# Key pages of a paged cache: fetched into a pool of their own instead of the weight ring

## The chip, the cores and the metric

One Trainium2 chip, one of its cores. The metric is the device time of one execution in microseconds (us), lower is better. A core has TensorE (matmuls), VectorE, ScalarE, GpSimd, and SyncE (SP), which here only issues transfers. In rows of the profile these are PE (and PEld for its weight loads), DVE, ACT, POOL and SP.

## The reference, cut to what matters

One layer of a decoder on 256 prompt tokens and 8 sequences of 4 new tokens, 288 columns in all. The keys of the 8 sequences' past lie in a cache of pages (128 rows of 8 heads x 128 values, 512 KB), which a page table picks: 64 pages.

```python
def ffn_half(h, g, wg, wu, wd):
    hn = rms_norm(h, g)
    return h + 0.5 * ((jax.nn.silu(hn @ wg) * (hn @ wu)) @ wd)
...
    hp = ffn_half(hp, norm_ffn1[l], w_ffn1_gate[l], w_ffn1_up[l], w_ffn1_down[l])
    cb, u, q, k, v, logf = mixer_in(hp, norm_mix[l], w_in[l], b_f[l])
...
    k_past = cache_k[page_table].reshape(DB, P, N_HEADS, HEAD_DIM)
    s = jnp.einsum('bqhd,bkhd->bhqk', q, k_all, preferred_element_type=jnp.float32) * SCALE
```

After the first FFN come the mixer (projections, a short convolution, attention of prompt and samples), a second FFN of the same size, a small per-layer embedding and a last norm. All in float32.

## The kernel before

**Weights.** All matmuls keep float32 accuracy by splitting each operand into a high and a low part and adding three products (L298, L299, L300). A weight tile, 512 rows x 256 columns, 512 KB, is loaded by SP into `wraw`. ScalarE rounds half of it to `whi` (L265), VectorE subtracts that for `wlo` (L266). There are 8 raw tiles (tag `raw`) and 5 pairs of halves. A step of the program uses one weight tile: 2 halves, 24 matmuls.

**The FFN.** A pair of output blocks is four steps over w_gate, then four over w_up. On a gate's end VectorE scales it (`tg`, L358), ScalarE applies the silu (`sg`, L360) and GpSimd multiplies by the norm's factor (`sr`, L362). On the up's end VectorE multiplies (`hd`, L367) and splits (`hl`, L370). After 3 or 4 pairs, the down steps add to `h` (L380).

**Key pages.** The keys must be turned before they can be used. While the first FFN runs, `k_turn(j)` handles page j: GpSimd gathers it by row indices `idx` into a tile `page` (L250), VectorE transposes it by blocks of 32 x 32 into `kt` (L460), and GpSimd writes `kt` with four transfers to `KD` in DRAM (L462). The mixer loads `KT` from `KD` (L247, SP). A page takes one of the 8 raw tiles, like a weight, and one place in the list of loads that runs 8 ahead (`load_upto`). The 64 calls are put among the steps of the FFN, 3.2 steps apart, by numbers at L475.

**The order.** Each engine runs its own queue in order and waits at an instruction until what it needs is there. Which order that is, is settled when the program is built: a scheduler places the instructions, close to the order in which they are written but not the same, so a moved call can move others. TensorE's order is the same before and after. Memory is taken by pools that are opened and closed as a stack from two ends (`opened`, `closed`). The pool `kt` on the right, from step 200 on, holds `KT`.

Of the kernel before, what the change touches and what calls it, by code (L numbers as in the profile page):

```python
# [16 lines left out]
F32 = mybir.dt.float32  # L17
# [8 lines left out]
P = 128  # L26
# [3 lines left out]
DB = 8  # L30
# [4 lines left out]
NH = 8  # L35
CB = 8
PAGES = 8
# [12 lines left out]
TSTEP = 16  # L50
# [38 lines left out]
def build(nc, tc, ctx, A, O):  # L89
    def pool(name, bufs=1, to=ctx, **k):  # L90
        return to.enter_context(tc.tile_pool(name=name, bufs=bufs, reuse_waits="tile", **k))

    v, s, g, pe, sy = nc.vector, nc.scalar, nc.gpsimd, nc.tensor, nc.sync
# [25 lines left out]
    h = cst.tile([P, KT, NT], F32, name="h")  # L119
# [39 lines left out]
    idx = cst.tile([P, 64], I32, name="idx")  # L159
# [73 lines left out]
    steps = []  # L233
# [39 lines left out]
    def page(src, j):  # L273
        return dict(kind="p", src=src, rows=idx[:, j:j + 1])
# [114 lines left out]
    W = {}  # L389

    def opened(name, side="left"):
        st = ExitStack()
        W[name] = (pool(name, to=st, side=side), st)

    def closed(name):
        W.pop(name)[1].close()
# [54 lines left out]

    KD = drp.tile([DB * PAGES // 2, P, 2, 4, NH * 32], F32, name="KD")

    def k_turn(j):

        its = [page(A["cache_k"], j)]

        def fn():
            t = W["f1"][0].tile([P, 4, NH, 32], F32, name="kt", tag="kt", bufs=2)
            v.transpose(t, its[0]["tile"].rearrange("p (h d c) -> p d h c", d=4, c=32))  # L460
            for i in range(4):
                g.dma_start(KD[j // 2, :, j % 2, i].rearrange("(d c) n -> c d n", c=32),  # L462
                            t[32 * i:32 * i + 32].rearrange("c d h r -> c d (h r)"))
        return (its, fn)

    def later_loads():
        t = load_gains(["norm_mix", "norm_ffn2", "norm_ple", "norm_final", "norm_conv_out", "norm_attn_out", "conv_w"], 16, sy)
# [1 line left out]
        defer(lambda: turn_gains(*t), 20)  # L469

    steps.insert(14, ([], lambda: closed("xs")))
    steps.insert(200, ([], lambda: opened("kt", "right")))
    steps.insert(44, ([], later_loads))
    for j in reversed(range(DB * PAGES)):
        steps.insert(66 + TSTEP * j // 5, k_turn(j))  # L475

    warm = cst.tile([P, 1], F32, name="warm")
    v.memset(warm, 1.0)
# [695 lines left out]
```

## Time and profile before

| | us |
|---|---|
| median of 3 runs | 2425.11 (2424.34 to 2426.46) |
| the profiled execution | 2432.94 |
| its span, first to last instruction | 2431.2 |
| TensorE busy | 2375.8 |
| VectorE busy | 1427.1 |
| GpSimd busy | 503.4 |
| transposes of key pages, 64 | 79.7 |
| fetches of key pages, 64 | 76.3 |
| writes to KD, 256 | 142.8 |

The profiled execution is one run of its own and a little longer than the runs timed without a profile. A group's busy time sums what its instructions took on their engine. For a transfer that is the time to issue it; its landing is told apart.

### The profile page before, as it was taken

How to read it: one execution, taken by the hardware profiler on the slowest of the kernel's cores; microseconds unless marked ns; L12 is line 12 of the kernel's file. 1: busy time of each engine (PE TensorE's matmuls, PEld its weight loads, DVE VectorE, ACT ScalarE, POOL GpSimd, SP SyncE). 2: the span in 40 equal slices, each digit the busy share in tenths (PEclk: the TensorE clock that was granted, in tenths of full speed). 3: DMA queues.
4: the chain of work that ended last, by engine and by line, in shares of the span. 5: the costliest groups of instructions: out<-in, count | busy, mean ns of one | idle time of the engine just before them, and what ended most of it. 6: DMA issues, size and time to landing. Idle time of an engine off the chain costs nothing.

```text
span 2431.2 us, 46137 instructions
## 1 busy us (share of the span) xinstructions
PE 2375.8 (98%) x17856; PEld 2298.6 (95%) x17856; DVE 1427.1 (59%) x2588; ACT 1052.2 (43%) x1858; POOL 503.4 (21%) x688
## 2 busy tenths in 40 slices
PE   8999999999999999999999999999999999999997
PEld 8999999999999999888877899999999999999997
DVE  6556655556565577555555685555555555555765
ACT  5443343343443354333334454444444444444554
POOL 2003432333333312111444410000000000000100
PEclk9999999999999999999999999999999999999998
DMA  7457878777777755898787754545555555555542
GB/s 229 154 177 260 295 249 273 239 256 256 243 262 252 245 182 165 295 304 305 244 301 258 258 163 147 177 151 179 165 165 165 166 165 165 165 165 165 165 153 83
DMA packets 410704, 510.85 MB, mean 210 GB/s; under 512 B 22236, under 2 KB 379316, under 8 KB 406356
## 3 DMA queue, kind: packets, MB, share of 16 engines
q1 hardware_dynamic: 376596, 401.43, 52.2%
q0 software_dynamic: 33664, 106.13, 12.4%
q8 instruction: 140, 2.29, 0.4%
q14 instruction: 80, 0.66, 0.1%
q10 hardware_dynamic: 224, 0.34, 0.1%
HBM read 469.19 MB, written 38.63 MB: 209 GB/s over the span
## 4 chain that ended last, share of the span: by engine, by line
PE 71%; DMA 9%; issue 4%; DVE 3%; POOL 1%; ACT 0%; DVEq 0%; POOLq 0%; ACTq 0%
PE mm L298 22%; PE mm L300 22%; PE mm L299 21%; DMA page<-in_cache_k_dram,idx 6%; DMA KD<-kt 2%; PE va L719 1%; PE va L776 1%; DVE wlo L266 1%; POOL KD L462 1%; DMA page<-in_cache_v_dram,idx 1%; DVE kt L460 1%; PE va L298 1%; PE va L300 1%; PE va L299 1%; ACT whi L265 0%
## 5 line engine op out<-in xcount | busy, mean ns | idle before, releaser
L266 DVE TENSOR_TENSOR wlo<-wraw,whi 128x512 fp32r<-128x512 f32 x1384 | 964.3, 706 | 645.1 <-ACT whi L265 601.8
L265 ACT ACTIVATE whi<-wraw 128x512 fp32r<-128x512 f32 x1384 | 862.0, 630 | 994.3 <-PE mm L299 930.6
L298 PE MATMUL mm<-xh,whi 128*128 128x288 f32 x3712 | 1110.5, 299 | 5.5 <-DVE hd L367 3.5
L300 PE MATMUL mm<-xh,wlo 128*128 128x288 f32 x3712 | 1094.2, 295 | 10.2 <-DVE wlo L266 10.2
L299 PE MATMUL mm<-xl,whi 128*128 128x288 f32 x3712 | 1097.1, 296 | 0.0
L298 PEld LDWEIGHTS mm<-xh,whi 128*128 128x128 f32 x3712 | 697.6, 188 | 30.1 <-ACT whi L265 16.1
L300 PEld LDWEIGHTS mm<-xh,wlo 128*128 128x128 f32 x3712 | 700.8, 189 | 12.2 <-DVE wlo L266 12.1
L299 PEld LDWEIGHTS mm<-xl,whi 128*128 128x128 f32 x3712 | 699.0, 188 | 0.1
L298 PE MATMUL mm<-hh,whi 128*128 128x288 f32 x1408 | 419.4, 298 | 11.3 <-DVE h L380 10.0
L300 PE MATMUL mm<-hh,wlo 128*128 128x288 f32 x1408 | 415.4, 295 | 3.5 <-DVE wlo L266 3.5
L299 PE MATMUL mm<-hl,whi 128*128 128x288 f32 x1408 | 416.7, 296 | 0.0
L298 PEld LDWEIGHTS mm<-hh,whi 128*128 128x128 f32 x1408 | 265.2, 188 | 13.9 <-DVE h L380 12.3
L300 PEld LDWEIGHTS mm<-hh,wlo 128*128 128x128 f32 x1408 | 266.4, 189 | 4.0 <-DVE wlo L266 4.0
L299 PEld LDWEIGHTS mm<-hl,whi 128*128 128x128 f32 x1408 | 265.8, 189 | 0.1
L362 POOL TENSOR_TENSOR sr<-sg,rs 128x288 f32<-128x288 f32 x88 | 72.3, 822 | 909.5 <-ACT sg L360 908.7
L462 POOL DMA_DIRECT2D KD<-kt x256 | 142.8, 563 | 319.8 <-DVE kt L460 318.4
L460 DVE STREAM_TRANSPOSE kt<-page 128x1024 f32<-128x1024 f32 x64 | 79.7, 1245 | 169.5 <-DMA page<-in_cache_k_dram,idx 108.0
L230 POOL TENSOR_TENSOR acc<-acc,sq 128x288 f32<-128x288 f32 x66 | 56.7, 860 | 265.2 <-ACT sq L229 220.9
L380 DVE SCALAR_TENSOR_TENSOR h<-mm,h 128x288 f32<-128x288 f32 x192 | 86.3, 451 | 17.6 <-PE mm L300 17.1
L250 POOL DMA_INDIRECT page<-in_cache_k_dram,idx x64 | 76.3, 1192 | 86.1 <-DVE wlo L266 66.3
L369 ACT ACTIVATE hh<-hd 128x288 fp32r<-128x288 f32 x88 | 39.2, 445 | 118.7 <-DVE hd L367 118.7
L360 ACT ACTIVATE sg<-tg 128x288 f32<-128x288 f32 x88 | 39.1, 445 | 118.8 <-DVE tg L358 118.8
(294 smaller groups left out, 1540.9 us busy)
## 6 DMA issues: line engine op xcount, KB each, us to landing
wraw<-in_w_ffn_gate_dram SPq DMA_DIRECT2D x176, 512.0 KB, 4.2
wraw<-in_w_ffn_up_dram SPq DMA_DIRECT2D x176, 512.0 KB, 3.8
wraw<-in_w_ffn_down_dram SPq DMA_DIRECT2D x160, 512.0 KB, 3.7
wraw<-in_w_in_dram SPq DMA_DIRECT2D x96, 512.0 KB, 5.0
KD<-kt POOLq DMA_DIRECT2D x256, 128.0 KB, 5.3
KT<-KD SPq DMA_DIRECT2D x32, 1024.0 KB, 7.2
wraw<-in_w_out_dram SPq DMA_DIRECT2D x32, 512.0 KB, 5.0
wraw<-in_w_ple_gate_dram SPq DMA_DIRECT2D x32, 512.0 KB, 3.7
```

Source lines behind the costliest of these rows:

```text
L230: (v if k >= KT - last_on_v else g).tensor_tensor(acc, acc, sq, ALU.add)
L250: g.indirect_dma_start(out=t, out_offset=None, in_=it["src"], in_offset=bass.IndirectOffsetOnAxis(ap=it["rows"], axis=0))
L265: s.activation(hi, x, AF.Copy)
L266: v.tensor_tensor(lo, x, hi.bitcast(F32), ALU.subtract)
L298: pe.matmul(o, hi[:, j % 2, w], xh, start=f, stop=False)
L299: pe.matmul(o, hi[:, j % 2, w], xl, start=False, stop=False)
L300: pe.matmul(o, lo[:, j % 2, w], xh, start=False, stop=l)
L362: g.tensor_tensor(r, u, rs, ALU.mult)
L369: s.activation(H["hi"][:, k, :], t, AF.Copy)
L380: v.scalar_tensor_tensor(h[:, k, :], o, 0.5, h[:, k, :], ALU.mult, ALU.add)
L460: v.transpose(t, its[0]["tile"].rearrange("p (h d c) -> p d h c", d=4, c=32))
L462: g.dma_start(KD[j // 2, :, j % 2, i].rearrange("(d c) n -> c d n", c=32), t[32 * i:32 * i + 32].rearrange("c d h r -> c d (h r)"))
```

## The change

Pages are no longer items of the load list and no longer use raw tiles. A new pool `kg`, on the right, holds four page tiles and three `kt` tiles (before there were two, in the FFN's own pool). `k_fetch(j)` gathers a page into `kg`; `k_turn(0)` fetches pages 0, 1 and 2, every later `k_turn(j)` fetches page j + 2 and then transposes page j. The calls begin at step 50 instead of 66, again 3.2 steps apart. Pool `kg` is opened at step 46 and closed at step 258; pool `kt` opens there instead of at step 200.

```diff
-        its = [page(A["cache_k"], j)]
-
-        def fn():
-            t = W["f1"][0].tile([P, 4, NH, 32], F32, name="kt", tag="kt", bufs=2)
-            v.transpose(t, its[0]["tile"].rearrange("p (h d c) -> p d h c", d=4, c=32))
-            for i in range(4):
-                g.dma_start(KD[j // 2, :, j % 2, i].rearrange("(d c) n -> c d n", c=32),
-                            t[32 * i:32 * i + 32].rearrange("c d h r -> c d (h r)"))
-        return (its, fn)
+    KG = {}
+
+    def k_fetch(j):
+        KG[j] = W["kg"][0].tile([P, NH * P], F32, name="kg", tag="kg", bufs=4)
+        g.indirect_dma_start(out=KG[j], out_offset=None, in_=A["cache_k"],
+                             in_offset=bass.IndirectOffsetOnAxis(ap=idx[:, j:j + 1], axis=0))
...
+        for i in range(3) if j == 0 else (j + 2,):
+            if i < DB * PAGES:
+                k_fetch(i)
+        t = W["kg"][0].tile([P, 4, NH, 32], F32, name="kt", tag="kt", bufs=3)
+        v.transpose(t, KG.pop(j).rearrange("p (h d c) -> p d h c", d=4, c=32))
+        for i in range(4):
+            g.dma_start(KD[j // 2, :, j % 2, i].rearrange("(d c) n -> c d n", c=32),
+                        t[32 * i:32 * i + 32].rearrange("c d h r -> c d (h r)"))
...
-    steps.insert(200, ([], lambda: opened("kt", "right")))
     steps.insert(44, ([], later_loads))
+    steps.insert(50 + TSTEP * 13, ([], lambda: (closed("kg"), opened("kt", "right"))))
     for j in reversed(range(DB * PAGES)):
-        steps.insert(66 + TSTEP * j // 5, k_turn(j))
+        steps.insert(50 + TSTEP * j // 5, ([], lambda j=j: k_turn(j)))
+    steps.insert(46, ([], lambda: opened("kg", "right")))
```

The lines of the changed kernel stand 6 or 7 lower: its fetch is L458, its transpose L467, its writes to KD L469.

On GpSimd, at the first pages, before:

```order
L362 TENSOR_TENSOR sr<-sg,rs 128x288 x9
L250 DMA page<-in_cache_k_dram,idx 128x1024
L362 TENSOR_TENSOR sr<-sg,rs 128x288
L462 DMA KD<-kt 32x4x256 x3
L250 DMA page<-in_cache_k_dram,idx 128x1024
L462 DMA KD<-kt 32x4x256 x4
L250 DMA page<-in_cache_k_dram,idx 128x1024
L462 DMA KD<-kt 32x4x256
```

and after the change, at the same place:

```order
L362 TENSOR_TENSOR sr<-sg,rs 128x288 x6
L458 DMA kg<-in_cache_k_dram,idx 128x1024 x4
L469 DMA KD<-kt 32x4x256 x3
L362 TENSOR_TENSOR sr<-sg,rs 128x288 x2
L469 DMA KD<-kt 32x4x256 x5
L458 DMA kg<-in_cache_k_dram,idx 128x1024
L469 DMA KD<-kt 32x4x256 x4
L458 DMA kg<-in_cache_k_dram,idx 128x1024
L469 DMA KD<-kt 32x4x256 x4
L362 TENSOR_TENSOR sr<-sg,rs 128x288
L458 DMA kg<-in_cache_k_dram,idx 128x1024
```

Before, one fetch stands between the writes of two pages, and the fetch of the next page comes behind the first writes of the last one. After, four fetches go out ahead of the first write to KD, and from then on a fetch follows each page's four writes; the fetch of page 6, the last row, stands behind an sr.

On VectorE, from the writing of `idx` on, before:

```order
L167 TENSOR_SCALAR idx<-ptb,consts 128x64
L266 TENSOR_TENSOR wlo<-wraw,whi 128x512 x6
L358 TENSOR_TENSOR tg<-mm,rs 128x288
L266 TENSOR_TENSOR wlo<-wraw,whi 128x512
L358 TENSOR_TENSOR tg<-mm,rs 128x288
L266 TENSOR_TENSOR wlo<-wraw,whi 128x512 x7
```

and after:

```order
L167 TENSOR_SCALAR idx<-ptb,consts 128x64
L266 TENSOR_TENSOR wlo<-wraw,whi 128x512 x3
L467 STREAM_TRANSPOSE kt<-kg 128x1024
L266 TENSOR_TENSOR wlo<-wraw,whi 128x512
L467 STREAM_TRANSPOSE kt<-kg 128x1024
L266 TENSOR_TENSOR wlo<-wraw,whi 128x512 x2
L467 STREAM_TRANSPOSE kt<-kg 128x1024
L358 TENSOR_TENSOR tg<-mm,rs 128x288
L266 TENSOR_TENSOR wlo<-wraw,whi 128x512
L358 TENSOR_TENSOR tg<-mm,rs 128x288
L266 TENSOR_TENSOR wlo<-wraw,whi 128x512 x3
L467 STREAM_TRANSPOSE kt<-kg 128x1024
```

The transposes begin 3 wlo behind `idx`; before, the first came 26 wlo behind it. Over all pages, the first transpose stands behind 103 wlo and the last behind 487 before, behind 80 and 391 after: mostly 6 wlo between two transposes before (4 to 8), and 4 to 6 after but for the first few.

On SP, the first loads of KT after the change, in the down steps of a later group:

```order
L242 DMA wraw<-in_w_ffn_down_dram 128x4x256 x9
L247 DMA KT<-KD 128x2048
L242 DMA wraw<-in_w_ffn_down_dram 128x4x256
L247 DMA KT<-KD 128x2048
L242 DMA wraw<-in_w_ffn_down_dram 128x4x256 x2
L247 DMA KT<-KD 128x2048
L242 DMA wraw<-in_w_ffn_down_dram 128x4x256 x4
```

Before, these three stood behind weight tiles 68, 95 and 120; now behind tiles 217, 218 and 220. The other loads of KT are where they were.

## Rows read from the trace of the kernel before

**Rows 1.** The page: busy time, granted clock in 40 slices, the split's costliest group.

```profile
PE 2375.8 (98%) x17856; PEld 2298.6 (95%) x17856; DVE 1427.1 (59%) x2588; ACT 1052.2 (43%) x1858; POOL 503.4 (21%) x688
...
PEclk9999999999999999999999999999999999999998
...
L266 DVE TENSOR_TENSOR wlo<-wraw,whi 128x512 fp32r<-128x512 f32 x1384 | 964.3, 706 | 645.1 <-ACT whi L265 601.8
```

**Rows 2.** Two stretches of 650 us; columns in the first line.

```profile
core 0: us, PE busy (x) PEld busy (x) DVE busy (x) ACT busy (x) POOL busy (x), PEclk, DMA share, GB/s
200.00:850.00 650.00, 619.53 (x4533) 612.03 (x4532) 385.18 (x600) 259.29 (x443) 236.42 (x342) 0.99 0.78 257
1500.00:2150.00 650.00, 650.00 (x4877) 650.00 (x4876) 352.05 (x584) 281.76 (x470) 25.98 (x32) 1.00 0.53 165
```

**Rows 3.** The first and the last of five half-speed stretches, columns as above.

```profile
222.60:226.00 3.40, 3.29 (x14) 3.29 (x14) 1.71 (x4) 0.87 (x2) 0.45 (x2) 0.50 1.02 341
...
632.20:635.60 3.40, 3.40 (x15) 3.12 (x14) 2.31 (x5) 1.91 (x5) 1.32 (x2) 0.50 0.95 300
```

**Rows 4.** Waits from 200 to 850 us: total us, times, longest.

```profile
DVE kt L460 <- DMA page<-in_cache_k_dram,idx: 105.8, 39, 6.3
...
POOL page L250 <- DVE wlo L266: 63.2, 43, 5.2
...
DVE kt L460 <- DMA KD<-kt: 46.7, 15, 6.5
...
DVE kt L460 <- issue: 14.7, 7, 3.7
...
PE mm L300 <- DVE wlo L266: 13.7, 10, 2.2
...
PE mm L298 <- DVE h L380: 11.5, 11, 2.3
...
PE mm L298 <- DVE hd L367: 4.9, 5, 2.7
```

**Rows 5.** GpSimd in order of time: start, us, instruction.

```profile
473.54 1.03 POOL L250 DMA_INDIRECT page<-in_cache_k_dram,idx  x1 [0.30 <-issue]
```

**Rows 6.** VectorE's transposes at 403 and 480 us, with the idle time before.

```profile
403.67 1.25 DVE L460 STREAM_TRANSPOSE kt<-page 128x1024 f32<-128x1024 f32 x1 [2.95 <-DMA page<-in_cache_k_dram,idx]
...
480.61 1.25 DVE L460 STREAM_TRANSPOSE kt<-page 128x1024 f32<-128x1024 f32 x1 [4.57 <-DMA page<-in_cache_k_dram,idx]
```

**Rows 7.** TensorE after these two transposes.

```profile
405.31 0.40 PE L298 MATMUL mm<-hh,whi 128*128 128x288 f32 x1 [1.06 <-DVE h L380]
...
482.25 0.61 PE L298 MATMUL mm<-xh,whi 128*128 128x288 f32 x1 [2.68 <-DVE hd L367]
482.66 0.44 PE L299 MATMUL mm<-xl,whi 128*128 128x288 f32 x1
```

**Rows 8.** Tile page while key pages pass: fetches, transposes, landings.

```profile
L250 POOL DMA_INDIRECT page<-in_cache_k_dram,idx x64: 1012/1182/1547, 176.5 to 837.9; - x64
L460 DVE STREAM_TRANSPOSE kt<-page x64: 1232/1245/1248, 181.0 to 844.4; 128x1024 f32<-128x1024 f32 x64
...
DMA to landing us min/median/max: 4.4/5.6/8.6
```

**Rows 9.** The tensor KD in the same time.

```profile
L462 POOL DMA_DIRECT2D KD<-kt x256: 550/552/639, 182.6 to 847.6; - x128
...
DMA to landing us min/median/max: 3.0/5.3/7.8
```

**Rows 10.** A gate's product: VectorE's tg, then GpSimd's sr.

```profile
466.80 0.45 DVE L358 TENSOR_TENSOR tg<-mm,rs 128x288 f32<-128x288 f32 x1
...
467.86 0.82 POOL L362 TENSOR_TENSOR sr<-sg,rs 128x288 f32<-128x288 f32 x1 [0.98 <-ACT sg L360]
```

**Rows 11.** Two stretches of the mixer, columns as in rows 2.

```profile
1000.00:1050.00 50.00, 50.00 (x437) 43.93 (x436) 23.97 (x53) 15.16 (x24) 7.64 (x12) 1.00 0.92 309
1200.00:1250.00 50.00, 49.43 (x363) 41.08 (x361) 19.96 (x40) 12.72 (x21) 21.32 (x24) 1.00 0.94 331
```

**Rows 12.** The list of DMA issues: value pages, count, us to landing.

```profile
page<-in_cache_v_dram,idx POOLq DMA_INDIRECT x64, 6.2
```

## The prediction

> **What bounds the kernel now.** I first read the page. TensorE is busy 98% of the span and holds full clock nearly throughout [rows 1], so the only thing to win is time in which it stands still. The change touches the first FFN, so I looked there.
>
> Two stretches of 650 us with the same kind of work, one in the first FFN while key pages pass, one in the second FFN without pages [rows 2]. The second runs 4877 matmuls, so one takes 650 / 4877 = 0.1333 us. The first runs 4533. The 344 missing ones are 344 x 0.1333 = **45.9 us**, the most that this change can return. Idle time is 650 - 619.5 = 30.5 us of it. Five stretches of 3.4 us at granted clock 0.50 (1.2 GHz) follow directly on gaps; the first has 14 matmuls and the last 15 [rows 3], against 3.4 / 0.1333 = 25.5 at the full 2.4 GHz: 5 x 11 x 0.1333 = 7.3 us. The remaining 8 us go in refilling after the gaps, of which the waits name 26 [rows 4].
>
> What opens the gaps is in the waits of that stretch [rows 4]: VectorE's transposes wait 105.8 us for their page, 46.7 us for KD writes (they free the two kt tiles) and 14.7 us for nothing the profile names. TensorE waits for wlo, h and hd, all VectorE's work that stands in line behind a transpose. One case: GpSimd issues a page fetch at 473.54 us, and VectorE stands still for 4.57 us, until it has landed, in front of the transpose at 480.61 us [rows 5, 6]. Then TensorE has a 2.68 us gap, ended by hd, the instruction behind the transpose, and starts again at half speed: 0.44 us instead of 0.29 a matmul [rows 7]. At 403.67 us the wait is 2.95 us and TensorE's gap 1.06 us [rows 6, 7]. Wait plus transpose is 5.82 us in one case and 4.20 us in the other; the gap is shorter by 3.14 us both times. So VectorE can be held for **3.1 us** before TensorE notices, and a transpose that doesn't wait (1.25 us) costs nothing.
>
> **The change, part by part.** A chunk (a step of four row blocks of weights) is 24 matmuls, 3.2 us, and brings two wlo, so one wlo stands for 12 matmuls, 1.6 us. I count places in VectorE's order in wlo.
>
> *Where the fetch stands.* Before, fetch j goes out behind the transpose of page j-1 and waits until a raw tile is free (GpSimd waited 63.2 us for wlo there [rows 4]); page and transpose are mostly 6 wlo, 9.6 us, apart, and the landing alone takes 5.6 us in the median, up to 8.6 us [rows 8]. After, four fetches go out together, and fetch j+3 stands behind the KD writes of page j: 12 to 16 wlo, 19 to 26 us, ahead of its transpose. With that the 105.8 us of waits for pages go, but for the two places below.
>
> *Three kt tiles for two.* Transpose j needs the KD writes of page j-3: 1.25 + 4 x 0.55 + landing 5.3 us in the median, 7.8 us at most [rows 9] = 8.8 to 11.3 us, against 15 wlo = 24 us. The 46.7 us go too.
>
> *A new wait: the gate's product.* sr (L362) stands in GpSimd's queue between KD writes and fetches, and queued behind it are those, and VectorE behind them. From tg to the end of sr it takes 1.9 us (tg starts at 466.80 us, sr at 467.86 us and takes 0.82 us [rows 10]); with a fetch of 5.6 us behind it 7.5 us, with three KD issues between 9.1 us. Nine fetches (pages 6, 21, 24, 27, 40, 43, 46, 59, 62) have only 4 to 6 wlo, 6.4 to 9.6 us, between that tg and their transpose. They come up to 1.1 us late, less than the 1.85 us (3.1 - 1.25) that do no harm. If every landing took 8.6 us, nine waits of 2.5 to 4.1 us would leave about 12 us of gaps, and with four half-speed stretches of 1.5 us some 18 us. I take the low end, **2 us**: at DMA share 0.94 the value pages landed in 6.2 us [rows 11, 12], 0.6 us more than here.
>
> *The start.* The page indices are written only 3 wlo, 4.8 us, ahead of the first transpose; the quickest fetch landed 4.4 us after its issue, the median one 5.6 us [rows 8], so it is at most a us late. Transposes 0 to 2 stand within 3 wlo, and transpose 3 comes 7 wlo (11.2 us) after transpose 0 and needs all its KD writes, the last of them behind two sr: tg 4 wlo later, then 1.9 + 0.8 + 0.55 + 5.3 us, 15 us in all. It is 3 to 4 us late, with its own 1.25 us a gap of 1 to 2 us. Bounds 0 and 5 us; I take **2 us**, and **2 us** for one stretch at half speed.
>
> *The pace.* VectorE's order now puts 63 pages in 311 wlo instead of 384, so 7.9 us a page at full speed. Per page GpSimd has 1.18 + 4 x 0.55 + about half an sr (0.4) = 3.8 us. Each transfer of its queue waits for the transfer eight places ahead: 5 of 8 places a page at 5.6 us are 3.5 us, 5.4 us if all took 8.6 us. Traffic: a page moves 2 x 0.524 MB, 133 GB/s, beside the 165 GB/s of weights: 298 GB/s. Without pages the share is 0.53, so pages took 0.78 - 0.93 x 0.53 = 0.29 for 257 - 0.93 x 165 = 104 GB/s [rows 2]; 133 GB/s make 0.37, in all **0.90**. In the mixer 309 GB/s ran at 0.92 with TensorE busy throughout [rows 11]. Cost nothing, covered by eight weight tiles of lead (25 us).
>
> *KT loads.* The first three move on SP from the early FFN to the point after the last transpose, since kt's memory is free only when the kg pool is closed. The first of them stands at half-tile 418, which SP reaches about when wlo 402 is done; the last KD write lands about 5.5 wlo after transpose 63 (wlo 391), so at 397. No weight waits behind it; without that cover there are still eight tiles of lead. The memsets of strip and qn move on GpSimd behind the last page, where nothing waits.
>
> *Sum.* 45.9 - 2 - 2 - 2 = 40 us (39.9). From the profiled execution: 2432.94 - 40 = 2393 us. The median of the runs lies 7.8 us below that execution: 2425.11 - 40 = **2385 us**.
>
> **Rivals.**
> 1. *The waits stay, at half size.* Landings grow with the share, sr arrives late in more places, and GpSimd passes its lateness on. For it: the late fetches have little slack, and a single 4 us block costs 1 us. Against: the other 55 have 7 wlo or more. With about 20 us left, 2425 - 26 = 2399 to 2410 us.
> 2. *Slower: the page loop can't keep 7.9 us.* VectorE is in order, so if a page needs p us, the 311 wlo take 63 p. It breaks even at 7.9 + 45.9 / 63 = 8.6 us. For it: a page took (844.4 - 181.0) / 63 = 10.5 us before [rows 8]. At 9.5 us it would cost 63 x 0.9 = 55 us: 2480 us. Against: these 10.5 us hold an order of 6.1 wlo (9.8 us) and the waits; the parts of the loop are 3.8, 3.5 and 8.8 / 3 = 2.9 us.
> 3. *Nothing changes: gaps come from something else.* TensorE's waits name wlo, h and hd [rows 4], so if VectorE alone were too slow, they would stay, 2425 us. Against: it is busy 385 of 650 us [rows 2], and in the second FFN, without transposes, 352.
> 4. *Issues held by VectorE.* If each of the nine late fetches goes out one transpose (1.25 us) later, they make 9 x 1.25 = 11 us of gaps: 2396 us. For it: fetch issues spread from 1012 to 1547 ns [rows 8]. Against: KD issues take 550 to 639 ns beside the same work of VectorE [rows 9], a spread far below the 0.71 us of a wlo [rows 1]. A rule says that it would be so: while VectorE runs certain copies, a transfer issued on GpSimd cannot write its descriptors (the Trainium skill, "SBUF — State Buffer", the box on the "DVE blocks DMA" trap). The KD rows don't bear it out for this kernel.
>
> **How the numbers follow.** 0.68 for the forecast (30 to 46 us won, 2379 to 2395 us), 0.10 for rival 1, 0.12 for rival 2, 0.06 for rival 3, 0.04 for rival 4. The range goes from the ceiling (2425 - 46, less a us of scatter) to the middle of rival 1 and a little more: **2378 to 2408 us**. The forecast's own is 2379 to 2395 us. A measurement here tells about 0.2%, 5 us, from no change: faster 0.82, same 0.06, slower 0.12.
>
> **What would show it.** In the new profile: transposes from about 142 us, about 7.9 us apart, done near 640 us; their waits for pages under 15 us; 4800 or more matmuls in 650 us of the page stretch; at most two stretches at half clock; DMA share about 0.9 while pages pass. Wrong would be: transposes more than 8.6 us apart with VectorE waiting for KD or kg (rival 2); landings above 8 us (rival 1); gaps with no transpose ahead (rival 3).

## The result and the profile after

The changed kernel takes 2391.97 us (median of 4 runs, 2387.86 to 2396.56) where the kernel before takes 2425.78 us in the runs beside it (2424.34 to 2435.15). The ratio is 0.9853, with a 95% interval of 0.9822 to 0.9884: 1.5% faster, by 33.8 us in the medians. 2385 us was predicted, in a range from 2378 to 2408. The profiled execution after takes 2396.56 us, 36.4 us less than the one before.

Five stretches of the changed kernel, columns as in [rows 2]: the one compared there, all pages, the start of the pages, and in it the one stretch at half speed.

```profile
200.00:850.00 650.00, 650.00 (x4878) 650.00 (x4877) 414.54 (x645) 286.04 (x487) 219.72 (x324) 1.00 0.80 262
140.00:650.00 510.00, 505.60 (x3763) 504.67 (x3762) 335.22 (x508) 217.55 (x368) 233.55 (x343) 0.99 0.89 292
150.00:200.00 50.00, 45.60 (x313) 44.67 (x312) 32.55 (x47) 19.33 (x34) 26.41 (x39) 0.90 0.85 283
153.60:163.80 10.20, 7.85 (x29) 7.15 (x30) 8.37 (x12) 2.67 (x5) 5.73 (x9) 0.50 0.81 256
0.00:50.00 50.00, 43.94 (x263) 38.42 (x264) 34.16 (x73) 29.47 (x61) 14.90 (x19) 1.00 0.75 236
```

Two stretches of the kernel before, to set beside them:

```profile
0.00:50.00 50.00, 43.47 (x274) 38.03 (x275) 35.83 (x74) 29.94 (x62) 15.51 (x22) 1.00 0.77 240
140.00:200.00 60.00, 60.00 (x453) 60.00 (x452) 33.86 (x55) 26.52 (x46) 11.79 (x15) 1.00 0.65 206
```

The first row answers [rows 2]: 4878 matmuls for 4533, so TensorE never stands still there. That is 345 x 0.1333 = 46.0 us won, as much as the stretch without pages allows. The third row has what is lost: 313 matmuls where 50 / 0.1333 = 375 fit, 62 x 0.1333 = 8.3 us; 50 - 45.60 = 4.4 us of it is idle time, the other 3.9 us the stretch of 10.2 us at granted clock 0.50 (1.2 GHz). Before, TensorE was busy throughout from 140 to 200 us (453 matmuls in 60 us). The last row has 11 matmuls less than the same stretch of before (274), 1.5 us, ahead of anything that the change touches. 46.0 - 8.3 - 1.5 = 36.2 us: the two profiled executions differ by 36.4.

The waits from 140 to 700 us (total us, times, longest), answering [rows 4]:

```profile
DVE kt L467 <- DMA kg<-in_cache_k_dram,idx: 22.3, 10, 6.5
...
DVE kt L467 <- DMA KD<-kt: 6.7, 3, 3.2
...
DVE idx L167 <- DMA ptb<-in_page_table_dram: 4.6, 1, 4.6
...
PE mm L300 <- DVE wlo L266: 3.6, 2, 3.2
...
PE mm L298 <- DVE tg L358: 0.8, 1, 0.8
```

VectorE waits 22.3 us for pages (105.8 before) and 6.7 us for KD writes (46.7 before). TensorE has three gaps left, all at the start. Tile kg, then KD's landings, answering [rows 8, 9]:

```profile
L458 POOL DMA_INDIRECT kg<-in_cache_k_dram,idx x64: 937/1021/1442, 145.5 to 641.5; - x64
L467 DVE STREAM_TRANSPOSE kt<-kg x64: 1230/1237/1247, 152.9 to 651.9; 128x1024 f32<-128x1024 f32 x64
...
DMA to landing us min/median/max: 5.5/6.8/8.0
```

```profile
L469 POOL DMA_DIRECT2D KD<-kt x256: 550/552/616, 154.4 to 663.4; - x128
...
DMA to landing us min/median/max: 2.4/5.6/8.1
```

64 transposes pass in 499 us (663 before), (651.9 - 152.9) / 63 = 7.9 us apart. A fetch lands after 6.8 us in the median (5.6 before), and still waits are fewer: by the starts of the 64 fetches and transposes in the trace it goes out 11.6 us ahead in the median (6.2 to 21.4; before 5.9, from 4.5 to 8.8). These leads run to the start of the transpose, so they hold its wait too. Until VectorE stands in front of the transpose a fetch has 3.4 us before, 2.2 us less than its landing takes in the median, and 11.6 us after. The start, on VectorE, GpSimd and TensorE in order of time:

```profile
139.06 0.69 DVE L266 TENSOR_TENSOR wlo<-wraw,whi 128x512 fp32r<-128x512 f32 x1
144.33 0.26 DVE L167 TENSOR_SCALAR idx<-ptb,consts 128x64 int32<-128x64 int32 x1 [4.58 <-DMA ptb<-in_page_table_dram]
144.50 1.89 DVE L266 TENSOR_TENSOR wlo<-wraw,whi 128x512 fp32r<-128x512 f32 x3
152.90 1.25 DVE L467 STREAM_TRANSPOSE kt<-kg 128x1024 f32<-128x1024 f32 x1 [6.51 <-DMA kg<-in_cache_k_dram,idx]
154.07 0.65 DVE L266 TENSOR_TENSOR wlo<-wraw,whi 128x512 fp32r<-128x512 f32 x1
155.12 1.25 DVE L467 STREAM_TRANSPOSE kt<-kg 128x1024 f32<-128x1024 f32 x1 [0.40 <-DMA kg<-in_cache_k_dram,idx]
```

```profile
145.50 1.32 POOL L458 DMA_INDIRECT kg<-in_cache_k_dram,idx  x1 [55.54 <-DMA wraw<-in_w_ffn_gate_dram]
```

```profile
154.78 0.61 PE L300 MATMUL mm<-xh,wlo 128*128 128x288 f32 x1 [3.22 <-DVE wlo L266]
...
156.99 0.61 PE L300 MATMUL mm<-xh,wlo 128*128 128x288 f32 x1 [0.41 <-DVE wlo L266]
...
159.09 0.61 PE L298 MATMUL mm<-xh,whi 128*128 128x288 f32 x1 [0.77 <-DVE tg L358]
```

VectorE stands 4.58 us in front of `idx`, because the page table hasn't landed. Then three wlo are ready and take 1.89 us together, and it stands 6.51 us for page 0, fetched at 145.50 us, 7.4 us ahead of its transpose. The wlo behind that transpose ends TensorE's gap of 3.22 us.

### The profile page after: what moved, and what is told of

Same layout as the page of the kernel before. It is cut to its first block, busy times and chain, and to the rows that moved or that the text cites. A ratio compares the mean times of both kernels' runs of the same rounds, so it can differ in the third digit from the quotient of the medians.

```text
span 2394.7 us, 46026 instructions
## 1 busy us (share of the span) xinstructions
PE 2365.7 (99%) x17856; PEld 2294.7 (96%) x17856; DVE 1430.9 (60%) x2588; ACT 1055.6 (44%) x1858; POOL 498.6 (21%) x688
## 4 chain that ended last, share of the span: by engine, by line
PE 93%; DMA 4%; issue 1%; DVE 1%; POOL 1%; ACT 0%; SPq 0%; POOLq 0%; DVEq 0%; ACTq 0%
PE mm L298 29%; PE mm L300 29%; PE mm L299 28%; DMA page<-in_cache_v_dram,idx 1%; PE va L726 1%; PE va L783 1%; PE va L298 1%; PE va L300 1%; PE va L299 1%; DMA wraw<-in_w_in_dram 1%; DMA bk<-FP 0%; POOL page L250 0%; DMA kg<-in_cache_k_dram,idx 0%; DMA wraw<-in_w_out_dram 0%; DMA xa<-in_x_prompt_dram 0%
## 5 line engine op out<-in xcount | busy, mean ns | idle before, releaser
L265 ACT ACTIVATE whi<-wraw 128x512 fp32r<-128x512 f32 x1384 | 864.5, 630 | 989.0 <-PE mm L299 915.0
L469 POOL DMA_DIRECT2D KD<-kt x256 | 142.5, 562 | 80.6 <-DVE kt L467 60.6
L467 DVE STREAM_TRANSPOSE kt<-kg 128x1024 f32<-128x1024 f32 x64 | 79.2, 1238 | 29.0 <-DMA kg<-in_cache_k_dram,idx 22.3
L458 POOL DMA_INDIRECT kg<-in_cache_k_dram,idx x64 | 71.6, 1118 | 74.5 <-DMA wraw<-in_w_ffn_gate_dram 55.5
```

What stands on the lines that cost most here:

```text
L265: s.activation(hi, x, AF.Copy)
L458: g.indirect_dma_start(out=KG[j], out_offset=None, in_=A["cache_k"], in_offset=bass.IndirectOffsetOnAxis(ap=idx[:, j:j + 1], axis=0))
L467: v.transpose(t, KG.pop(j).rearrange("p (h d c) -> p d h c", d=4, c=32))
```

## The experiments

Three causes were to be told apart. **L**: what counts is how far ahead of its transpose a fetch is issued (its lead), because VectorE, in order, holds up everything behind a transpose that waits. **R**: what counts are raw tiles, which pages no longer take from the weights. **K**: what counts is the third `kt` tile. Besides, what remains at the start was put down to how close behind `idx` the first transposes stand. Each kernel was timed in 3 rounds beside the kernel before on the same chip.

**e1_before_kept**: the kernel before, with its transpose held at its written place (the scheduler may move others around it). Pages stay in the raw tiles and `kt` has two.

```diff
-            v.transpose(t, its[0]["tile"].rearrange("p (h d c) -> p d h c", d=4, c=32))
+            tc.keep_in_program_order(v.transpose(t, its[0]["tile"].rearrange("p (h d c) -> p d h c", d=4, c=32)))
```

> The kernel before with one edit: the transposes of key pages keep their written order on VectorE, so that they no longer move up to just behind their fetch. Pages still share the raw tiles with the weights, and there are still two kt tiles. In the listed order the distance from one transpose to the next page's fetch grows from mostly 6 wlo to 9 to 20 wlo (14 to 32 us). Theory L (what counts is how far ahead of its transpose a fetch is issued): the waits for pages go without any pool of their own, 2380 to 2392 us, transposes waiting under 15 us for pages. Rival R (the page must leave the raw tiles): about 2425 us as before. Rival K (the third kt tile is what counts): 2415 to 2425 us, with transposes waiting some 40 us for KD writes.

Measured: 2384.0 us (2383.12 to 2387.26) against 2428.24, ratio 0.9818 (0.9785 to 0.9852). The stretch of [rows 2], then tile page and the wait of its fetches from 140 to 860 us:

```profile
200.00:850.00 650.00, 650.00 (x4878) 650.00 (x4877) 432.46 (x657) 290.04 (x495) 248.00 (x361) 1.00 0.84 273
```

```profile
L250 POOL DMA_INDIRECT page<-in_cache_k_dram,idx x64: 973/1019/1447, 176.7 to 801.7; - x64
L460 DVE STREAM_TRANSPOSE kt<-page x64: 1229/1239/1246, 202.9 to 817.6; 128x1024 f32<-128x1024 f32 x64
...
DMA to landing us min/median/max: 4.1/5.6/9.0
```

```profile
POOL page L250 <- DVE wlo L266: 151.6, 39, 10.6
```

No gap is left, and no transpose waits at all, with neither of the change's tiles. GpSimd waits for raw tiles more than before (151.6 us, 66.3 before in the same 720 us), and that costs nothing: a fetch now goes out 10.4 to 26.7 us (median 19.7) ahead of its transpose. L holds; neither R nor K is needed. The order that the scheduler made on its own, with the transpose moved up close behind its fetch, was the whole loss of the kernel before in that stretch.

**e7_before_three_kt**: the kernel before with the third tile alone.

```diff
-            t = W["f1"][0].tile([P, 4, NH, 32], F32, name="kt", tag="kt", bufs=2)
+            t = W["f1"][0].tile([P, 4, NH, 32], F32, name="kt", tag="kt", bufs=3)
```

> The kernel before with three kt tiles instead of two, everything else as it was. Rival K (the third kt tile is what counts): the 46.7 us of waits for KD writes go and with them some 15 us of the time, 2405 to 2415 us. Theory L: those waits become waits for the page that is late anyway, 2418 to 2430 us, with the waits for pages at 105 us or more.

Measured: 2429.63 us (2427.68 to 2431.84) against 2425.51, ratio 1.0015 (1.0 to 1.0029). The waits from 200 to 850 us:

```profile
DVE kt L460 <- DMA page<-in_cache_k_dram,idx: 138.9, 50, 5.6
...
DVE kt L460 <- DMA KD<-kt: 8.5, 3, 4.4
```

The wait for KD goes (46.7 to 8.5 us), and the wait for pages behind it grows by nearly as much (105.8 to 138.9 us). K alone gives nothing.

**e3_two_kt**: the change with two `kt` tiles.

```diff
-        t = W["kg"][0].tile([P, 4, NH, 32], F32, name="kt", tag="kt", bufs=3)
+        t = W["kg"][0].tile([P, 4, NH, 32], F32, name="kt", tag="kt", bufs=2)
```

> The changed kernel with two kt tiles instead of three. In the order the pace stays 5.0 wlo a page, so transpose j stands 10 wlo (16 us) behind transpose j-2, whose KD writes need 8.8 to 11.4 us. Theory L: 2388 to 2396 us, no difference, waits for KD under 10 us. Rival K: some 45 us of waits for KD writes come back, and the time goes to 2405 to 2425 us.

Measured: 2391.48 us (2390.85 to 2392.07), ratio 0.9846 (0.9813 to 0.9878), the time of the change itself. VectorE's waits for KD are 5.8 us in 5. The third tile is worth nothing here either. The edit isn't clean, though: the scheduler's order changed with it, and fetches go out 17.9 us ahead of their transposes in the median instead of 11.6.

**e8_six_raw**: the change with six raw tiles, so that the weights have no more of them than a kernel that lends two to pages.

```diff
-RAW = 8
+RAW = 6
```

> The changed kernel with six raw tiles instead of eight, so that weights have no more of them than before the change, when one or two were held by pages. Rival R (the gain is the weights' longer lead): it goes, 2410 to 2425 us. Theory L: 2388 to 2398 us, no wait of TensorE for weights in the first FFN.

Measured: 2413.94 us (2412.66 to 2418.47), ratio 0.9949 (0.993 to 0.9968); as a total L's expectation was missed by 16 us, and the total lies in R's range. But the loss isn't in the first FFN:

```profile
200.00:850.00 650.00, 650.00 (x4877) 649.99 (x4876) 413.92 (x644) 286.49 (x488) 218.93 (x324) 1.00 0.81 262
1100.00:1350.00 250.00, 241.47 (x1724) 193.62 (x1723) 130.88 (x310) 87.06 (x178) 114.17 (x137) 1.00 0.75 252
```

The last of these stretches in the change itself, where both kernels reach the mixer at the same time (the gather of L563 stands at 876.0 us here and at 876.9 us in the change):

```profile
1100.00:1350.00 250.00, 246.60 (x1844) 204.83 (x1843) 142.25 (x341) 94.99 (x196) 115.37 (x140) 1.00 0.80 273
```

While key pages pass, the weights run at full speed with six tiles, so R falls there. In the mixer 1724 matmuls pass instead of 1844, 120 x 0.1333 = 16 us: there the value pages still share the raw tiles, and ScalarE's waits for the weights of L265 grow from 20.2 to 69.0 us. My expectation had looked at the first FFN alone.

**e4_one_kg**: the change with one page tile, and no written lead. A fetch can only go out behind the transpose of the page before it.

```diff
-        KG[j] = W["kg"][0].tile([P, NH * P], F32, name="kg", tag="kg", bufs=4)
+        KG[j] = W["kg"][0].tile([P, NH * P], F32, name="kg", tag="kg", bufs=1)
...
-        for i in range(3) if j == 0 else (j + 2,):
+        for i in (j,):
```

> The changed kernel with one page tile in the pool of its own and the fetch written in the call of its own page, so that fetch j waits for transpose j-1. The distance to the next transpose is 6 to 8 wlo (9.6 to 12.8 us), about as little as before the change, and it has to hold a transpose (1.25 us), mostly the KD writes (2.2 us) and a landing (5.6 to 6.8 us): 9 to 10.3 us. Theory L: the short distances are late by under 1 us and the rest not at all; small gaps at most, 2390 to 2402 us. Rival R (own tiles are enough, however short the lead): 2388 to 2396 us. If the waits of before come back in full, 2420 us and more, then L has the needed lead too short.

Measured: 2389.01 us (2387.35 to 2396.85), ratio 0.9846 (0.981 to 0.9883). Its waits, and VectorE and TensorE at its only two gaps:

```profile
DVE kt L467 <- DMA kg<-in_cache_k_dram,idx: 56.3, 37, 5.0
```

```profile
161.38 1.25 DVE L467 STREAM_TRANSPOSE kt<-kg 128x1024 f32<-128x1024 f32 x1 [4.98 <-DMA kg<-in_cache_k_dram,idx]
...
679.04 1.25 DVE L467 STREAM_TRANSPOSE kt<-kg 128x1024 f32<-128x1024 f32 x1 [2.96 <-DMA kg<-in_cache_k_dram,idx]
```

```profile
163.25 0.40 PE L300 MATMUL mm<-xh,wlo 128*128 128x288 f32 x1 [2.40 <-DVE wlo L266]
...
680.69 0.40 PE L298 MATMUL mm<-hh,whi 128*128 128x288 f32 x1 [1.06 <-DVE h L380]
```

Wait plus transpose less gap is 2.96 + 1.25 - 1.06 = 3.15 us in the second, as in the trace of before, and 4.98 + 1.25 - 2.40 = 3.83 us in the first. 35 waits, with a mean of 1.5 us over all 37 and up to 4.1 us, cost nothing. So a lead need not cover the landing; how much may be lacking depends on the place. Call wait plus transpose less gap the hold, the time that VectorE stood before TensorE noticed. In the kernel before, gaps follow 24 transposes. In 12 of them TensorE waits for the h, hd or tg right behind the transpose, and the hold is 3.1 us, so that 3.1 - 1.25 = 1.85 us may be lacking. In ten it waits for a wlo, and the hold is 3.8 to 5.5 us. The other two, 1.4 and 1.7 us, stand behind a transpose that had waited too.

The lead is 7.0 us in the median (5.9 to 8.6) with landings of 6.6 us; without the waits it is 6.2 us, where the kernel before has 3.4. The transposes stand 6 to 8 wlo apart (before 4 to 8, mostly 6), and no fetch waits for a raw tile (1.5 us a wait in [rows 4]). That fits L: some 3 us more of lead, and the time of the change itself. A run that parts the own tile from the wider spacing and the third `kt` tile was not made.

**e6_no_written_lead**: the change with its four page tiles, but each page fetched in its own call.

```diff
-        for i in range(3) if j == 0 else (j + 2,):
+        for i in (j,):
```

> The changed kernel with each page fetched in the call that transposes it, not two calls ahead; the pool of four page tiles stays. In the order hardly anything changes: a fetch still goes out 12 to 20 wlo ahead of its transpose, because the tiles are free and the scheduler moves it up. Theory L (the distance in the queues counts): 2386 to 2396 us. If the written two pages ahead count: waits for pages as before, 2410 us and more.

Measured: 2397.96 us (2396.13 to 2399.55), ratio 0.9878 (0.9861 to 0.9895), 2 us above what was expected. Transposes now come in groups of mostly three or four, 3.0 us from one to the next in the median, and the lead falls to 9.4 us in the median (4.7 at least). Waits for pages are 29.5 us in 17, with three small gaps (2.2 us) besides those of the start. So most of the gain stays without the written two pages ahead. Whether they are worth the 6 us between the medians (2397.96 - 2391.97) isn't shown: the two ratios' intervals overlap. Nor is it the number of tiles, since e4 has its gain with one.

**e5_early_table**: the change with the page table loaded 14 steps earlier.

```diff
-    steps.insert(44, ([], later_loads))
+    steps.insert(30, ([], later_loads))
```

> The changed kernel with the page table loaded 14 steps earlier and nothing else. The transposes move with it: the first stands 2 wlo behind the writing of the row indices, as close as before the edit (3). If the loss at the start comes from that closeness (fetch to landing 7 us against 3 to 5 us), it stays, and the time is 2388 to 2396 us, with a wait of 5 to 7 us in front of the first transpose. If it comes from the late table alone, it goes: 2380 to 2386 us.

Measured: 2391.96 us (2389.76 to 2392.81), ratio 0.9851 (0.9834 to 0.9867). VectorE at the start:

```profile
111.94 0.26 DVE L167 TENSOR_SCALAR idx<-ptb,consts 128x64 int32<-128x64 int32 x1 [0.69 <-DMA ptb<-in_page_table_dram]
...
119.85 1.25 DVE L467 STREAM_TRANSPOSE kt<-kg 128x1024 f32<-128x1024 f32 x1 [4.57 <-DMA kg<-in_cache_k_dram,idx]
```

The wait for the table is gone, but the scheduler moved the first transposes up with `idx`, two wlo behind it, and page 0 is late as before: 3.0 us of gaps, 6.8 us at half speed. It is the closeness, not the late table, that costs.

**e9_kept_only** and **e2_kept_early_table**: the change with its transposes held at their written place; the second also loads the table 8 steps earlier.

```diff
-        v.transpose(t, KG.pop(j).rearrange("p (h d c) -> p d h c", d=4, c=32))
+        tc.keep_in_program_order(v.transpose(t, KG.pop(j).rearrange("p (h d c) -> p d h c", d=4, c=32)))
...
-    steps.insert(44, ([], later_loads))
+    steps.insert(36, ([], later_loads))
```

> The changed kernel with the transposes kept in written order and the page table loaded where it was. The first transpose stands 8 wlo (12.8 us) behind the writing of the row indices; fetch issue and landing need about 8.5 us. If the distance is what the start lacks: no gap after a page, 2381 to 2387 us, as with both edits. If the late table matters as well: a gap of its own at about 145 us, 2387 to 2392 us.

> The changed kernel with two edits against the loss at its start: the transposes keep their written order, so the first comes 18 wlo (29 us) behind the writing of the row indices instead of 3, and the page table is loaded 8 steps earlier. If the loss left is the start alone (a gap of 6 us and 10.2 us at half clock, together about 9 us), it goes: 2380 to 2385 us, and no wait of TensorE for VectorE's work in the first FFN. If it is something else in the profile's start, 2392 us as before the edits.

Measured: 2384.98 us (2383.21 to 2386.82), ratio 0.9824 (0.9792 to 0.9857), and 2384.05 us (2382.83 to 2386.38), ratio 0.9814 (0.9781 to 0.9846). Neither has a gap from 140 to 850 us. This stretch in the change and in e9, then VectorE at the start of e9:

```profile
140.00:850.00 710.00, 705.60 (x5263) 704.67 (x5262) 449.15 (x695) 309.16 (x526) 249.72 (x366) 0.99 0.80 263
140.00:850.00 710.00, 710.00 (x5327) 710.00 (x5327) 462.21 (x707) 316.55 (x538) 247.15 (x369) 1.00 0.85 265
```

```profile
144.56 0.26 DVE L167 TENSOR_SCALAR idx<-ptb,consts 128x64 int32<-128x64 int32 x1 [4.52 <-DMA ptb<-in_page_table_dram]
...
153.34 1.23 DVE L467 STREAM_TRANSPOSE kt<-kg 128x1024 f32<-128x1024 f32 x1
```

It waits as long for the table as the change does; eight wlo stand between `idx` and the first transpose instead of three, and nothing is lost: 64 matmuls more than in the change, 8.5 us. The lead is now 34 us in the median, and gives no more than the 20 us of e1.

**e10_first_kept**: only the first transpose is held, with the table 6 steps earlier; the others keep the scheduler's faster pace.

```diff
-        v.transpose(t, KG.pop(j).rearrange("p (h d c) -> p d h c", d=4, c=32))
+        d = v.transpose(t, KG.pop(j).rearrange("p (h d c) -> p d h c", d=4, c=32))
+        if j < 1:
+            tc.keep_in_program_order(d)
...
-    steps.insert(44, ([], later_loads))
+    steps.insert(38, ([], later_loads))
```

> The changed kernel with only the first transpose kept in written order and the page table loaded 6 steps earlier: the first transpose stands 15 wlo (24 us) behind the indices, all later ones at the pace of the change, 4.9 wlo a page, DMA share about 0.9. If the start is all that was left and the faster pace costs nothing: 2381 to 2387 us. If the faster pace has a price of its own beside the start: 2387 to 2394 us with gaps of TensorE later in the page stretch.

Measured: 2384.8 us (2384.78 to 2388.03), ratio 0.9825 (0.9794 to 0.9857), as e9. With transposes 7.9 us apart only one small gap is left (0.24 us). So the start was what the change lost against e9, and its pace costs nothing.

## Why the prediction was right, point by point

*Where the fetch stands* held. The page waits of 105.8 us fell to 22.3 us, where under 15 was named: 6.51 us of them stand in front of page 0, and of the other nine none opens a gap from 200 us on. e1 gives the same gain by the lead alone. The 3.1 us that VectorE can be held, read off two gaps, is that of a transpose with h or hd right behind it; e4 shows it again, and 3.83 us where wlo follow.

*Three kt tiles for two* was right in that the KD waits went (46.7 to 6.7 us), and wrong in crediting the tile with it: with two tiles (e3) they stay at 5.8 us, so here too it is the order that took them away, and the tile alone (e7) wins nothing.

*A new wait: the gate's product* was put at 2 us and cost none: from 200 to 850 us TensorE is busy for all of 650.00 us. The place was right, the sizes weren't. All nine pages named wait, but 0.6 to 3.5 us instead of up to 1.1, six of them longer than the 1.85 us that were to do no harm. (For pages 27 and 46 the profile names KD, but the page too landed only 0.1 us ahead of the transpose.) Page 62, and what stands behind it:

```profile
644.80 1.25 DVE L467 STREAM_TRANSPOSE kt<-kg 128x1024 f32<-128x1024 f32 x1 [3.50 <-DMA kg<-in_cache_k_dram,idx]
645.97 1.25 DVE L266 TENSOR_TENSOR wlo<-wraw,whi 128x512 fp32r<-128x512 f32 x2
647.14 0.45 DVE L367 TENSOR_TENSOR hd<-mm,sr 128x288 f32<-128x288 f32 x1
```

Their landings took 6.3 to 7.6 us for 5.6, and VectorE came up to 2 us sooner than counted at 1.6 us a wlo. By the hold of 3.1 us these six would have cost 6.7 us of gaps. They cost none: wlo stand between these transposes and the next hd, and in such places the hold was longer, up to 5.5 us in the kernel before. That two errors cancelled is luck.

*The start* is the step that was mis-sized: 2 us of gaps and 2 us at half speed were taken, and 4.4 and 3.9 us measured. Two things failed in it. The wait of `idx` for the page table was overlooked, though the kernel before has it too (3.89 us, without harm). And the cover was counted in TensorE's pace, 3 wlo as 4.8 us; but behind a held VectorE the wlo are all ready and pass in 1.89 us. So VectorE waited 6.51 us for page 0, where the prediction had the page a us late at most, and the first gap was 3.22 us. Transpose 3, on which the estimate went, was not the one that cost. e9, e2 and e10 take the first transpose away from `idx` and get 2384 to 2385 us, 7 to 8 us less than the change, and the 64 matmuls of e9's trace are 8.5 us: this term.

*The pace* came as worked out: 7.9 us apart, DMA share 0.89 for 0.90, the last transpose at 651.9 us for 640, since the first stood at 152.9 instead of 142.

*The rivals.* Half of the waits staying (1) and no change (3) are excluded by the 4878 matmuls. The page loop (2) kept its 7.9 us, below the 8.6 us at which it breaks even. Issues held by VectorE (4): KD issues take 550 to 616 ns beside VectorE's work, and the late fetches opened no gap. The rule of the Trainium skill is on copies that keep GpSimd from writing descriptors ("SBUF — State Buffer", the "DVE blocks DMA" trap). While pages pass, VectorE's work is two-input operations and transposes, apart from one copy of 0.3 us, so neither these KD rows nor those of before test it, and the prediction should not have read them so.

*Sum*: 45.9 - 2 - 2 - 2 = 40 us was predicted; 46.0 - 0 - 4.4 - 3.9 - 1.5 = 36.2 us is what the profiled executions show, and 33.8 us the medians, since the profiled execution of before lies 7.2 us above its median and that of after 4.6 us.

## What to carry to other kernels

Where an in-order engine feeds TensorE and also waits for a transfer, look first at how far ahead the transfer is issued in the queues as built, not as written: the scheduler had put each transpose close behind its fetch, and one line that held it in place was worth 44 us, more than a pool of their own for the pages gave. Measure how long the engine may stand (wait plus work less gap) at several gaps and not at two, since it depends on what stands behind the wait: 3.1 us here with h or hd, 3.8 to 5.5 us with wlo. Leave alone all waits below it. Behind an engine that has been held, count cover by the time that its ready work takes, not by the pace of the engine that it feeds.

## What the runs showed of the hardware

The stretch at half clock after the first gap lasted 10.2 us here, with two small gaps inside it, 10.2 us in e8 too, 6.8 us in e3, e5 and e6, and 3.4 us each in the kernel before. Not every gap has one: none followed the 2.40 us of e4. Pages in a pool of their own landed later, 6.8 us in the median at DMA share 0.89 and 6.6 us in e4 at 0.84, than e1's in the raw tiles, 5.6 us at the same 0.84; what makes the difference stays open. The DMA engines carried 292 GB/s for 510 us at share 0.89, and in that time no weight came late to ScalarE.
